# Transposed attention output, norm_ffn multiplied on the gathered rows with held weight loads, and x also given transposed

## The chip, the core and the metric

The kernel runs on one core of a Trainium2 chip. The metric is device time in microseconds (us) for one execution; the time before is the median of three runs. Five engines run side by side: PE (TensorE, matrix products and transposes), DVE (VectorE), ACT (ScalarE), POOL (GpSimd) and SP (SyncE, which here issues loads). Each engine runs its own instructions in order; they wait for one another and for DMA transfers by semaphores. PEld is the weight load of PE.

## The reference, cut to what is computed

One encoder block on 1024 tokens of width 1024:

```python
h = rms_norm(x, norm_mix)
z = h @ w_in                       # u | q | k | v, 512 columns each
A = multiscale_pool(u)             # 4 groups, windows 2/4/8/16
B = neighbourhood_attention(q, k, v)   # 8 heads of 64, a 16x64 grid of tokens
x = x + concat(A, B) @ w_out
h = rms_norm(x, norm_ffn)
aff = softmax(h @ w_router)        # 16 experts
gates, idx = top_k(aff.T, 128)     # each expert takes 128 tokens
ye = (silu(h[idx] @ w_gate) * (h[idx] @ w_up)) @ w_down
x = x + scatter_add(ye * gates)
x = x + sigmoid(rms_norm(x, norm_ple) @ w_ple_gate) * rms_norm(p @ w_ple_proj, norm_ple_post)
```

Everything is fp32.

## The kernel before, in words

A large product is made of three fast ones: both operands are split into a rounded part `hi` (ACT) and the rest `lo` (DVE, `split`, L83 to 88), and `mm3` (L90 to 97) issues hi·hi, lo·hi and hi·lo. So every weight and activation passes ACT and DVE once before PE can use it. PE's order is written out by hand: `run_block` issues the 8 groups of a product (k = 0 to 7), and ahead of group i the small pieces that a table gives for position i (8 stands behind the last group). PE therefore waits wherever a piece's input is late, and what stands behind the piece waits too. DVE, ACT and POOL are ordered by a scheduler. The stages:

1. **First projection** (u, L189 to 198). The tokens come in 8 groups u of 128 (16 grid rows by 8 columns). `load_x0` brings x by rows, `norm_x` takes the sum of squares, `turn_x` (L179) turns x by 8 PE transposes into PSUM and splits from there.
2. **Attention** in 32 blocks t = (pair of heads pr, group u). `pair_block` (L295) projects q, k and v of block t; beside it `side_at` (L407) puts `score` of block t-3 at position 0, its `turn_p` at 5 and 6 and its `blend` at 7 and 8, and `turn_qk` of block t-1 at 6. `score` (L334) multiplies q and k of two heads on the two row halves of the array (64 rows each); DVE adds the bias and finds the maximum, ACT takes exp and its sum. `turn_p` transposes the weights of a head (2 or 3 key groups of 128), and `blend` (L368) multiplies them by v: 128 tokens by 64 channels for each head, in plain fp32, then DVE takes the reciprocal of the sums and scales into `yas`, by tokens.
3. **Output projection and routing** for 8 row blocks (`out_block`). `prep` (L448) makes the transposed input `ct` of a block; the attention half is turned by 4 PE transposes per block into the PSUM buffer "t" and split. The last three attention blocks finish inside the first two output blocks. `route` computes the router's softmax; then `gained` (L531) multiplies the block's 1024 columns by norm_ffn on POOL and the row is stored in `hrow` with its affinities. Meanwhile DVE ranks the affinities (L580 to 631), and PE transposes `at` for it, in the same PSUM buffer "t".
4. **End of routing**: the last block's softmax and `gained`, the last ranking steps, the token lists, and the gather of expert 0's 128 rows (L928); beside it the units of `embed` (p @ w_ple_proj).
5. **Experts**: 16 of them, each 24 weight chunks of 1 MB (`load_chunk`), loaded by SP into raw slots of several pools (A 8, B 4, C 3, O, H), split by ACT and DVE into at most 4 `fhi`/`flo` pairs, used by 12 matmuls of 512 columns. Each expert's rows are gathered by POOL during the one before.
6. **Gate stage**, with norm_ple_post applied on DVE.

Of the kernel before, what the change touches and what calls it, by code (L numbers as in the profile page):

```python
# [41 lines left out]
NRC = 3  # L42
# [4 lines left out]
def block_kernel(ctx, tc, x, p, vecs, w_u_in, w_qkv, w_pool, bias_rows, w_out, w_router, w_gate, w_up,  # L47
# [118 lines left out]

    def load_x0(u):
        xts[u] = up.tile([P, D], F32, tag="x", name=f"x_{u}", bufs=3)
        for c in (slice(0, 512), slice(512, D)) if u == 0 else (slice(0, D),):
            SP.dma_start(xts[u][:, c], x_u[u][..., c])  # L170

    def norm_x(u):
        xt = xts[u]
        sq = up.tile([P, D], BF16, tag="sq", name=f"sq_{u}", bufs=1)
# [37 lines left out]
    load_x0(0)  # L212
# [17 lines left out]
    for u in range(NU):  # L230
        sides = {}
        if u + 1 < NU:
            sides[4] = [lambda u=u: turn_x(u + 1, 0)]
            sides[6] = [lambda u=u: turn_x(u + 1, 1)]
        if u:
            sides[3] = [lambda u=u: turn_u(u - 1)]
        if u + 1 < NU:
            sides.setdefault(6, []).append(lambda u=u: norm_x(u + 1))
        run_block(u_block(u), sides)
        if u + 3 < NU:  # L240
            load_x0(u + 3)
# [46 lines left out]
    vs, qs, qkns, sbs, PTs, pys, dens = {}, {}, {}, {}, {}, {}, {}  # L288
# [45 lines left out]
    def score(t):  # L334
# [72 lines left out]
    def side_at(t):  # L407
        sides = {}

        def at(i, f, *a):  # L410
            sides.setdefault(i, []).append(lambda: f(*a))
        if t == 0:
            at(4, turn_u, NU - 1)
        if t >= 3:
            at(0, score, t - 3)
            at(5, turn_p, t - 3, 0)
            at(6, turn_p, t - 3, 1)
            at(7, blend, t - 3, 0)
            at(8, blend, t - 3, 1)
        if 1 <= t <= NT:  # L420
            at(6, turn_qk, t - 1)
        return sides
# [25 lines left out]
    def prep(u):  # L448
# [67 lines left out]
    def softmax(u):  # L516
# [233 lines left out]
    for u in range(NU):  # L750
# [4 lines left out]
        if u == 0:  # L755
            at(0, score, NT - 3)
            at(2, turn_p, NT - 3, 0)
            at(2, turn_p, NT - 3, 1)
            at(3, turn_qk, NT - 1)
            at(4, blend, NT - 3, 0)  # L760
            at(4, blend, NT - 3, 1)
            at(4, score, NT - 2)
            at(6, turn_p, NT - 2, 0)
            at(6, turn_p, NT - 2, 1)
            at(6, score, NT - 1)
            at(7, blend, NT - 2, 0)
            at(7, blend, NT - 2, 1)
            at(8, turn_p, NT - 1, 0)
            at(8, turn_p, NT - 1, 1)
# [12 lines left out]
        if u == 1:  # L782
# [29 lines left out]
    fps = fps_st.enter_context(pool("fps", 2, space=PSUM))  # L812
    units = embed_units()
# [95 lines left out]
    def index(e):  # L909
# [15 lines left out]
        if e == 0:  # L925
# [3 lines left out]
                                      in_offset=bass.IndirectOffsetOnAxis(ap=ix[:, :1], axis=0))  # L929
        xes[e] = xe  # L930
# [98 lines left out]
    for e in range(E):  # L1029
# [16 lines left out]
        for kk in range(8):  # L1046
# [70 lines left out]
_INS = ['x', 'p', 'vecs', 'w_u_in', 'w_qkv', 'w_pool', 'bias_rows', 'w_out', 'w_router', 'w_gate', 'w_up',  # L1117
# [78 lines left out]
```

## Time and profile before

| what | us |
|---|---|
| median of 3 runs (lowest, highest) | 1672.84 (1672.43, 1674.53) |
| the profiled execution, its own time | 1677.14 |
| span of its trace | 1675.4 |
| PE, PEld busy | 1637.1, 1372.4 |
| DVE, ACT, POOL busy | 1347.9, 1152.5, 171.7 |
| mean granted clock of TensorE | 0.995 |

The profiled execution ran 1.74 us outside its span and 4.3 us over the median. Busy time of PE counts matmuls as the profile models them, which overlap; so the distance from one start to the next tells what an instruction costs in a run of them. The chain of waits that ended last lies on PE for 87% of the span.

### The profile page before, as it was taken

To read this page: it belongs to the slowest core of one execution; us is meant where nothing else is said; L and a number is where in the kernel's file an instruction comes from. 1 tells how busy PE (TensorE), PEld (TensorE's weight loads), DVE (VectorE), ACT (ScalarE), POOL (GpSimd) and SP (SyncE) were. 2 spreads that over 40 slices of the span, in tenths; PEclk is the share of its full clock that TensorE was granted. 3 is DMA by queue.
4 is the path that set the end of the run, shared out by engine and by line. 5 is a ranking of instruction groups with operands and counts; after the bars stand their busy time and mean duration, and the time that the engine had idled before them with its cause. 6 is when DMAs were issued, how large, how long until landed. Compare 5 with 4: busy or idle time off the path is not lost.

```text
span 1675.4 us, 22979 instructions
## 1 busy us (share of the span) xinstructions
PE 1637.1 (98%) x8181; PEld 1372.4 (82%) x8181; DVE 1347.9 (80%) x1870; ACT 1152.5 (69%) x1472; POOL 171.7 (10%) x215
## 2 busy tenths in 40 slices
PE   8999999998899999999999999999999999999998
PEld 6889998787778888888888888888888888888787
DVE  4474555448879999999999999999999999999932
ACT  6254555432388888888888888888888888888631
POOL 1111112243220000000000000000000000000200
PEclk9999999999999999999999999999999999999999
DMA  6301201263689999999999999999999999999121
GB/s 182 121 20 41 67 26 51 59 220 102 205 315 397 379 368 407 372 390 387 369 402 376 372 404 369 398 380 366 409 368 395 384 367 405 375 382 394 51 100 59
DMA packets 129266, 470.54 MB, mean 281 GB/s; under 512 B 9600, under 2 KB 14720, under 8 KB 129152
## 3 DMA queue, kind: packets, MB, share of 16 engines
q1 hardware_dynamic: 123120, 446.85, 70.8%
q0 software_dynamic: 6032, 22.23, 5.1%
q8 instruction: 64, 1.05, 0.3%
q14 instruction: 50, 0.41, 0.1%
HBM read 448.00 MB, written 21.04 MB: 280 GB/s over the span
## 4 chain that ended last, share of the span: by engine, by line
PE 87%; DVE 7%; POOL 1%; ACT 1%; issue 1%; DMA 1%; SPq 0%; DVEq 0%; ACTq 0%; POOLq 0%
PE pu L93 8%; PE pu L95 8%; PE pu L97 8%; PE pg L93 7%; PE pg L95 7%; PE pg L97 7%; PE pd L95 7%; PE pd L93 7%; PE pd L97 7%; PE proj L93 2%; DVE both L580 2%; PE proj L97 2%; PE proj L95 2%; PE py L374 2%; PE tr_h L937 2%; PE pq L95 2%
## 5 line engine op out<-in xcount | busy, mean ns | idle before, releaser
L86 DVE TENSOR_TENSOR flo<-fraw,fhi 128x1024 fp32r<-128x1024 f32 x766 | 913.6, 1221 | 70.2 <-ACT fhi L85 33.5
L85 ACT ACTIVATE fhi<-fraw 128x1024 fp32r<-128x1024 f32 x766 | 807.1, 1060 | 191.5 <-PE pd L95 71.7
L93 PE MATMUL pd<-fhi,hidT 128*128 128x512 f32 x508 | 160.9, 398 | 0.0
L93 PE MATMUL pg<-fhi,xeT 128*128 128x512 f32 x512 | 159.2, 392 | 0.8 <-ACT xeT L85 0.8
L93 PE MATMUL pu<-fhi,xeT 128*128 128x512 f32 x512 | 159.2, 392 | 0.0
L95 PE MATMUL pu<-fhi,xeT 128*128 128x512 f32 x512 | 158.0, 390 | 0.0
L95 PE MATMUL pg<-fhi,xeT 128*128 128x512 f32 x512 | 157.8, 389 | 0.0
L97 PE MATMUL pg<-flo,xeT 128*128 128x512 f32 x512 | 157.8, 389 | 0.0
L97 PE MATMUL pu<-flo,xeT 128*128 128x512 f32 x512 | 157.6, 389 | 0.0
L95 PE MATMUL pd<-fhi,hidT 128*128 128x512 f32 x508 | 157.1, 391 | 0.0
L97 PE MATMUL pd<-flo,hidT 128*128 128x512 f32 x508 | 156.8, 390 | 0.0
L97 PEld LDWEIGHTS pu<-flo,xeT 128*128 128x128 f32 x512 | 96.1, 188 | 20.4
L95 PEld LDWEIGHTS pg<-fhi,xeT 128*128 128x128 f32 x512 | 96.0, 188 | 20.4 <-DVE xeT L86 0.4
L95 PEld LDWEIGHTS pu<-fhi,xeT 128*128 128x128 f32 x512 | 96.1, 188 | 20.3
L97 PEld LDWEIGHTS pg<-flo,xeT 128*128 128x128 f32 x512 | 96.1, 188 | 20.1
L97 PEld LDWEIGHTS pd<-flo,hidT 128*128 128x128 f32 x508 | 95.3, 188 | 20.6
L95 PEld LDWEIGHTS pd<-fhi,hidT 128*128 128x128 f32 x508 | 95.3, 188 | 20.5
L93 PEld LDWEIGHTS pg<-fhi,xeT 128*128 128x128 f32 x512 | 94.8, 188 | 19.8 <-ACT xeT L85 1.1
L93 PEld LDWEIGHTS pu<-fhi,xeT 128*128 128x128 f32 x512 | 94.9, 188 | 18.8
L93 PEld LDWEIGHTS pd<-fhi,hidT 128*128 128x128 f32 x508 | 92.0, 188 | 16.4
L1022 POOL DMA_INDIRECT acc_rows<-ye,ix x16 | 26.6, 1660 | 764.3 <-ACT ye L1009 699.2
L93 PE MATMUL proj<-wph,xT 128*128 128x384 f32 x256 | 100.3, 392 | 0.0
(235 smaller groups left out, 2365.9 us busy)
## 6 DMA issues: line engine op xcount, KB each, us to landing
fraw<-in_w_gate_dram SPq DMA_DIRECT2D x128, 1024.0 KB, 7.3
fraw<-in_w_down_dram SPq DMA_DIRECT2D x128, 1024.0 KB, 9.3
fraw<-in_w_up_dram SPq DMA_DIRECT2D x127, 1024.0 KB, 7.7
x<-in_x_dram SPq DMA_DIRECT2D x15, 512.0 KB, 5.1
wp_raw<-in_w_qkv_dram SPq DMA_DIRECT2D x16, 384.0 KB, 4.0
h_rows<-x POOLq DMA_DIRECT2D x8, 520.5 KB, 3.8
wo_raw<-in_w_out_dram SPq DMA_DIRECT2D x8, 512.0 KB, 3.3
acc_rows<-x SPq DMA_DIRECT2D x8, 512.0 KB, 4.2
```

Of the source, the lines that this page charges most:

```text
L85: ACT.activation(hi, src, AF.Copy)
L86: return DVE.tensor_tensor(lo, src, hi.bitcast(F32), op=ALU.subtract)
L93: PE.matmul(outs[j], xh, wh[j], start=start, stop=False)
L95: PE.matmul(outs[j], xl, wh[j], start=False, stop=False)
L97: PE.matmul(outs[j], xh, wl[j], start=False, stop=stop)
L374: PE.matmul(pys[t][:, h], PTs[t, h][:, j * P:(j + 1) * P], vs[NU * pr + u0 + j][:, h * HD:(h + 1) * HD], start=(j == 0), stop=(j == u1 - u ...
L580: DVE.tensor_tensor(b[:, :, j], a[:, :, 0], a[:, :, 1], op=(ALU.max, ALU.min)[j])
L937: PE.transpose(pt[:, j, :], src[:, k * P:(k + 1) * P], ident)
L1022: return POOL.indirect_dma_start(out=acc, out_offset=bass.IndirectOffsetOnAxis(ap=idxs[e][:, :1], axis=0), in_=ye, in_offset=None, compute ...
```

## The change

- The host gives x a second time, transposed (`xt`). Each u loads both forms; `turn_x` splits straight from the loaded tile with no transposes. x itself serves the sum of squares alone, squared in place. The x buffers go from 3 to 2, the x loads of group u+2 follow block u.
- `blend` swaps its operands: v is the weight (128 rows, 64 columns), the transposed attention weights are the moving side (128 columns), and the two heads alternate on the two column halves of the array. Its output is already transposed, so `prep` splits it from SBUF. The division by the sums moves ahead of `turn_p`: per head a reciprocal and a `tensor_scalar` over the 128x384 weights on DVE; `ya` becomes a copy. Each piece gets one more block: `blend` of t-5 and `score` of t-3 at 1, `turn_p` of t-4 at 5 and 6, `turn_qk` at 7.
- `gained` is gone. The gathered rows are multiplied by norm_ffn in two halves of 512 columns, on DVE for expert 0 and on POOL for the 15 others. norm_ffn and norm_ple_post get buffers of their own; pool C has 2 slots.
- Weight loads: 4 A chunks are loaded in output block 2 (3 before) and then CCHH (CCCHH). None is issued between these and the token list of expert 0 (4 were, two of them behind `counted`); 4 follow it, and 4 further ones and norm_ple_post wait for a small transfer that reads the gathered rows of expert 0.
- A tile `bank_order` holds the order of the PSUM banks.

```diff
+    def load_xT(u):
+        raw_xT[u] = up.tile([P, KD, P], F32, tag="xr", name=f"xr_{u}")
+        n = 2 if u == 0 else 1
+        for h in range(n):
+            ks = slice(h * KD // n, (h + 1) * KD // n)
+            SP.dma_start(raw_xT[u][:, ks], xt[u][:, ks])
...
-        ACT.activation(sq, xt, AF.Square, accum_out=ssq)
+        ACT.activation(xts[u], xts[u], AF.Square, accum_out=ssq)
...
-        pt = ps.tile([P, 4, P], F32, tag="pt", name=f"xt_ps_{u}_{h}")
-        for k in range(4):
-            PE.transpose(pt[:, k, :], xts[u][:, (4 * h + k) * P:(4 * h + k + 1) * P], ident)
-        split(xT[u][:, 0, 4 * h:4 * h + 4], xT[u][:, 1, 4 * h:4 * h + 4], pt)
+        ks = slice(4 * h, 4 * h + 4)
+        split(xT[u][:, 0, ks], xT[u][:, 1, ks], raw_xT[u][:, ks])
...
             ACT.activation(sb[:, :n], sb[:, :n], AF.Exp, bias=nmx, scale=-1.0, accum_out=dens[t][:, h:h + 1])
+            rd = tiny.tile([P, 1], F32, tag="rd", name=f"rd_{pr}_{u}_{h}")
+            DVE.reciprocal(rd, dens[t][:, h:h + 1])
+            DVE.tensor_scalar(sb[:, :n], sb[:, :n], rd, None, op0=ALU.mult)
...
         for j in range(u1 - u0):
-            PE.matmul(pys[t][:, h], PTs[t, h][:, j * P:(j + 1) * P],
-                      vs[NU * pr + u0 + j][:, h * HD:(h + 1) * HD], start=(j == 0), stop=(j == u1 - u0 - 1))
-        if h == 1:
-            rd = tiny.tile([P, 2], F32, tag="rd", name=f"rd_{pr}_{u}")
-            DVE.reciprocal(rd, dens[t])
-            DVE.tensor_tensor(yas[u // 4][:, u % 4, pr * P:(pr + 1) * P].rearrange("p (a b) -> p a b", b=HD), pys[t],
-                              rd[:, :, None].to_broadcast([P, 2, HD]), op=ALU.mult)
+            for h in range(2):
+                hs = slice(h * HD, (h + 1) * HD)
+                PE.matmul(py[hs], vs[NU * pr + u0 + j][:, hs], PTs[t, h][:, j * P:(j + 1) * P],
+                          start=(j == 0), stop=(j == u1 - u0 - 1))
+        DVE.tensor_copy(yas[u // 4][:, u % 4, pr * P:(pr + 1) * P], py)
...
-            at(0, score, t - 3)
-            at(5, turn_p, t - 3, 0)
...
+                at(1, blend, t - 5)
+            at(1, score, t - 3)
...
-        pt = ps.tile([P, 4, P], F32, tag="t", name=f"yat_{u}", bufs=1)
-        for k in range(4):
-            PE.transpose(pt[:, k, :], yas[u // 4][:, u % 4, k * P:(k + 1) * P], ident)
-        split(ct[:, 0, 4:8], ct[:, 1, 4:8], pt)
+        split(ct[:, 0, 4:8], ct[:, 1, 4:8], yas[u // 4][:, u % 4].rearrange("p (k q) -> p k q", q=P))
...
-        gained(u)
         POOL.tensor_copy(x1s[u][:, D:D + E], affq[:, u, 0:E])
...
-    for which in "CCCHH":
+    gfb, gp = (fw.tile([P, D], F32, name=n) for n in ("gfb", "gp"))
+    bc_rows(gfb, norm_ffn[0], D)
+    for which in "CCHH":
         load_chunk(which)
-    ring += ["A"] * 5
...
-    with tc.issue_after(counted.ins):
-        feed()
-        feed()
...
+        for h in range(2):
+            hs = slice(h * 512, (h + 1) * 512)
+            (POOL if e else DVE).tensor_tensor(xe[:, hs], xe[:, hs], gfb[:, hs], op=ALU.mult)
...
+    mark = SP.dma_start(nc.dram_tensor("mark", (1, 16), F32, kind="Internal").ap(), xes[0][0:1, D:D + 16])
+    with tc.issue_after(mark.ins):
+        for _ in range(4):
+            load_chunk("A")
+        bc_rows(gp, norm_ple_post[0], D)
...
     with tc.issue_after(made.ins):
-        feed()
-        feed()
+        for _ in range(4):
+            feed()
```

The order of PE at the seam of two attention blocks, before (`py` is the blend, `s` the score, `proj` the projection; the names' last numbers are buffers):

```order
L374 MATMUL py_6_1383<-v_5_1043,PT_6_0_1361 128x64 [waits Activation_49]
L374 MATMUL py_6_1383<-v_6_1128,PT_6_0_1361 128x64
L374 MATMUL py_6_1383<-v_7_1213,PT_6_0_1361 128x64
L93 MATMUL proj_1_1322<-wph_3_1232,xT_208 128x384
L95 MATMUL proj_1_1322<-wph_3_1232,xT_208 128x384
L97 MATMUL proj_1_1322<-wpl_3_1233,xT_208 128x384
L374 MATMUL py_6_1383<-v_5_1043,PT_6_1_1370 128x64 [waits DVE_49]
L374 MATMUL py_6_1383<-v_6_1128,PT_6_1_1370 128x64
L374 MATMUL py_6_1383<-v_7_1213,PT_6_1_1370 128x64
L345 MATMUL s_7_0_1408<-kT,q_7_1291 128x256
```

and the same place in the changed kernel:

```order
L95 MATMUL proj_1_2711<-wph_0_2158,xT_199 128x384
L97 MATMUL proj_1_2711<-wpl_0_2159,xT_199 128x384
L384 MATMUL py_4_2715<-PT_4_0_2676,v_3_2255 64x128 [waits DVE_49,Activation_49]
L384 MATMUL py_4_2715<-PT_4_1_2685,v_3_2255 64x128 [waits DVE_49]
L384 MATMUL py_4_2715<-PT_4_0_2676,v_4_2341 64x128
L384 MATMUL py_4_2715<-PT_4_1_2685,v_4_2341 64x128
L384 MATMUL py_4_2715<-PT_4_0_2676,v_5_2427 64x128
L384 MATMUL py_4_2715<-PT_4_1_2685,v_5_2427 64x128
L351 MATMUL s_6_0_2724<-kT,q_6_2588 128x384 [waits Activation_49]
```

The two heads' products stood apart, each of them two key groups or three in a row with a group of `proj` between; now they alternate, three key groups by two heads, straight ahead of the score.

The order of PE where the output projection begins, before (`yat` is the transposed attention output, `po` the output projection):

```order
L374 MATMUL py_4_3299<-v_3_2966,PT_4_1_3286 128x64 [waits DVE_49]
L374 MATMUL py_4_3299<-v_4_3057,PT_4_1_3286 128x64
L374 MATMUL py_4_3299<-v_5_3139,PT_4_1_3286 128x64
L461 MATMUL yat_3351<-ident,ya_88 128x128 [waits DVE_49]
L461 MATMUL yat_3351<-ident,ya_88 128x128 x3
L345 MATMUL s_5_0_3361<-kT,q_5_3209 128x384 [waits Activation_49]
L345 MATMUL s_5_1_3362<-kT,q_5_3209 128x384
L345 MATMUL s_5_0_3361<-kT,q_5_3209 128x384
L345 MATMUL s_5_1_3362<-kT,q_5_3209 128x384
L345 MATMUL s_5_0_3361<-kT,q_5_3209 128x384
L345 MATMUL s_5_1_3362<-kT,q_5_3209 128x384
L93 MATMUL po_0_3358<-woh_2808,ct_3346 128x512 [waits Activation_49]
```

and in the changed kernel:

```order
L93 MATMUL proj_7_3252<-wph_3_2616,xT_515 128x384
L95 MATMUL proj_7_3252<-wph_3_2616,xT_515 128x384
L97 MATMUL proj_7_3252<-wpl_3_2617,xT_515 128x384
L93 MATMUL po_0_3369<-woh_2800,ct_3362 128x512 [waits PE_49,Activation_49]
L93 MATMUL po_1_3370<-woh_2800,ct_3362 128x512 [waits DVE_49,PE_49]
L95 MATMUL po_0_3369<-woh_2800,ct_3362 128x512 [waits Pool_49]
```

Blend, transposes and score that stood between the last `proj` and the first `po` are gone from there; both `po` buffers have the PSUM tag of `proj`.

The order of POOL at the gathers of experts 1 and 2, before:

```order
L928 DMA xe_5122<-h_rows,ix_5120 128x1041 [waits DVE_49]
L1022 DMA acc_rows<-ye_5550,ix_4883 1024x1024 [waits Activation_49]
L928 DMA xe_5724<-h_rows,ix_5722 128x1041 [waits DMASW0_49,DVE_49]
L1022 DMA acc_rows<-ye_6152,ix_5120 1024x1024 [waits DMASW3_49,Activation_49]
L928 DMA xe_6326<-h_rows,ix_6324 128x1041 [waits DMASW2_49,DVE_49]
```

and in the changed kernel:

```order
L923 DMA xe_5134<-h_rows,ix_5132 128x1041 [waits DVE_49]
L927 TENSOR_TENSOR xe_5134<-xe_5134,gfb 128x512 [waits DMAHW7_49,DMASW2_49]
L927 TENSOR_TENSOR xe_5134<-xe_5134,gfb 128x512
L1025 DMA acc_rows<-ye_5564,ix_4873 1024x1024 [waits DMAHW3_49,DMAHW5_49,DMAHW2_49,Activation_49]
L923 DMA xe_5738<-h_rows,ix_5736 128x1041 [waits DMAHW2_49,DMASW0_49,DVE_49]
L927 TENSOR_TENSOR xe_5738<-xe_5738,gfb 128x512 [waits DMASW4_49]
L927 TENSOR_TENSOR xe_5738<-xe_5738,gfb 128x512
```

Behind each gather stand two multiplications that wait for it to land, and the scatter of the expert before stands behind them.

## Rows read from the trace of the kernel before

**Rows 1.** Windows by stage: length, busy time of each engine (x instructions), PEclk, DMA share, GB/s

```profile
8.90:69.00 60.10, 56.24 (x277) 45.19 (x278) 24.89 (x46) 29.62 (x52) 5.96 (x16) 0.97 0.48 129
69.00:307.60 238.60, 228.99 (x1503) 211.50 (x1502) 137.12 (x377) 121.27 (x313) 42.67 (x62) 0.99 0.15 49
307.60:442.40 134.80, 124.22 (x661) 102.43 (x660) 90.64 (x357) 40.22 (x98) 43.66 (x54) 0.97 0.48 138
442.40:475.10 32.70, 29.97 (x154) 23.64 (x154) 23.34 (x98) 22.83 (x37) 13.21 (x24) 0.95 0.78 273
475.10:1572.00 1096.90, 1096.89 (x5120) 906.90 (x5120) 1025.27 (x931) 904.59 (x918) 52.03 (x32) 1.00 0.99 377
```

**Rows 2.** Waits of PE: line, awaited: us in total, times, longest us

```profile
PE pt L360 <- ACT sb L352: 7.2, 7, 2.0
PE at L589 <- DVE ct L86: 5.7, 3, 2.4
PE qkt L320 <- DVE qkn L312: 2.7, 2, 1.4
...
PE xt_ps L184 <- DMA x<-in_x_dram: 1.6, 1, 1.6
...
PE po L93 <- DVE qkn L312: 1.4, 1, 1.4
```

**Rows 3.** Groups by line, 8.9 to 69 us

```profile
L184 PE MATMUL xt_ps<-ident,x 128*128 128x128 f32 x56 | 8.4, 273 | 1.6 <-DMA x<-in_x_dram 1.6
```

**Rows 4.** Timeline of PE, 37.5 to 40.5 us: start, length, instruction

```profile
38.58 0.40 PE L97 MATMUL pu<-wul,xT 128*128 128x512 f32 x1
38.81 0.60 PE L184 MATMUL xt_ps<-ident,x 128*128 128x128 f32 x4
...
39.49 0.39 PE L95 MATMUL pu<-wuh,xT 128*128 128x512 f32 x1
```

**Rows 5.** Timeline of PE, 288.3 to 292.3 us

```profile
288.44 0.49 PE L360 MATMUL pt<-ident,sb 128*128 128x128 f32 x3
288.77 0.38 PE L320 MATMUL qkt<-ident,qkn 128*128 128x128 f32 x2
...
289.52 0.78 PE L374 MATMUL py<-v,PT 128*128 128x64 f32 x6
290.10 0.42 PE L93 MATMUL proj<-wph,xT 128*128 128x384 f32 x1
...
290.71 0.78 PE L374 MATMUL py<-v,PT 128*128 128x64 f32 x6
291.42 0.79 PE L345 MATMUL s<-kT,q 64*128 64x384 f32 x6
292.14 0.44 PE L93 MATMUL proj<-wph,xT 128*128 128x384 f32 x1
```

**Rows 6.** Timeline of PE, 266.5 to 268.2 us

```profile
266.62 0.62 PE L345 MATMUL s<-kT,q 64*128 64x256 f32 x6
267.17 0.44 PE L93 MATMUL proj<-wph,xT 128*128 128x384 f32 x1
```

**Rows 7.** Groups by line and shape, 69 to 307 us

```profile
L374 PEld LDWEIGHTS py<-v,PT 128*128 128x128 f32 x314 | 43.1, 192 | 0.6 <-ACT PT L363 0.3
...
L365 DVE COPY PT<-pt 128x384 f32<-128x384 f32 x22 | 12.2, 556 | 17.2 <-PE pt L360 17.2
...
L378 DVE RECIPROCAL rd<-den 128x2 f32<-128x2 f32 x29 | 4.8, 164 | 18.2 <-ACT sb L352 18.2
```

**Rows 8.** Line 533, `gained`: duration ns min/median/max, first and last start

```profile
L533 POOL TENSOR_TENSOR x<-x,gfb x8: 2378/2392/2435, 337.9 to 449.6; 128x1024 f32<-128x1024 f32 x8
```

**Rows 9.** Timeline of DVE, 382.2 to 387.5 us

```profile
382.69 2.09 DVE L526 TENSOR_SCALAR both<-ex,sm 128x16 f32<-128x16 f32 x1
```

**Rows 10.** Timeline of DVE, 449.1 to 453 us

```profile
449.19 0.22 DVE L526 TENSOR_SCALAR both<-ex,sm 128x16 f32<-128x16 f32 x1
```

**Rows 11.** The page's groups: busy, mean ns, idle time before

```profile
L86 DVE TENSOR_TENSOR flo<-fraw,fhi 128x1024 fp32r<-128x1024 f32 x766 | 913.6, 1221 | 70.2 <-ACT fhi L85 33.5
```

More of the change, by code (lines that the diff above doesn't have):

```diff
@@ L41, with block_kernel @@
 NRB = 4
-NRC = 3
+NRC = 2
 NH = 4
 @with_exitstack
-def block_kernel(ctx, tc, x, p, vecs, w_u_in, w_qkv, w_pool, bias_rows, w_out, w_router, w_gate, w_up,
+def block_kernel(ctx, tc, x, xt, p, vecs, w_u_in, w_qkv, w_pool, bias_rows, w_out, w_router, w_gate, w_up,
                  w_down, w_ple_gate, w_ple_proj, norm_ffn, norm_ple_post, edge, consts, out):
@@ L165, in load_u_w @@
         uwt.append((hi, lo))
+    raw_xT = {}
+    def load_xT(u):
[4 more added lines that the diff above has]
+            SP.dma_start(raw_xT[u][:, ks], xt[u][:, ks])
     def load_x0(u):
-        xts[u] = up.tile([P, D], F32, tag="x", name=f"x_{u}", bufs=3)
-        for c in (slice(0, 512), slice(512, D)) if u == 0 else (slice(0, D),):
-            SP.dma_start(xts[u][:, c], x_u[u][..., c])
+        xts[u] = up.tile([P, D], F32, tag="x", name=f"x_{u}")
+        SP.dma_start(xts[u], x_u[u])
     def norm_x(u):
-        xt = xts[u]
-        sq = up.tile([P, D], BF16, tag="sq", name=f"sq_{u}", bufs=1)
         ssq = tiny.tile([P, 1], F32, tag="ssq", name=f"ssq_{u}")
-        ACT.activation(sq, xt, AF.Square, accum_out=ssq)
+        ACT.activation(xts[u], xts[u], AF.Square, accum_out=ssq)
         rstd_of(ssq, D, 1, f"rstd_{u}", rx[:, u:u + 1])
@@ L211, in block_kernel @@
         POOL.memset(Us[i][:, :, S + PAD:], 0.0)
-    load_x0(0)
+    load_xT(0)
     SP.dma_start(vec, vecs)
@@ L222, in block_kernel @@
         load_u_w(kk)
-    load_x0(1)
+    load_x0(0)
     norm_x(0)
     first.close()
-    load_x0(2)
+    load_xT(1)
+    load_x0(1)
     cst = up.tile([P, 4 * P], F32, name="cst", bufs=1)
@@ L239, in block_kernel @@
         run_block(u_block(u), sides)
-        if u + 3 < NU:
-            load_x0(u + 3)
+        if u + 2 < NU:
+            load_xT(u + 2)
+            load_x0(u + 2)
         if u == 3:
@@ L286, in pool_mix @@
         ACT.activation(Ug, pp, AF.Copy, scale=pscale[:, g:g + 1])
-    vs, qs, qkns, sbs, PTs, pys, dens = {}, {}, {}, {}, {}, {}, {}
+    vs, qs, qkns, sbs, PTs, dens = {}, {}, {}, {}, {}, {}
     bias_t = {}
@@ L366, in turn_p, with blend @@
         PTs[t, h] = PT
-    def blend(t, h):
+    def blend(t):
         pr, u = divmod(t, NU)
         u0, u1, n = span(u)
-        if h == 0:
-            pys[t] = ps.tile([P, 2, HD], F32, tag="py", name=f"py_{pr}_{u}", bufs=1)
+        py = ps.tile([P, P], F32, tag="py", name=f"py_{pr}_{u}", bufs=1)
         for j in range(u1 - u0):
-            PE.matmul(pys[t][:, h], PTs[t, h][:, j * P:(j + 1) * P],
-                      vs[NU * pr + u0 + j][:, h * HD:(h + 1) * HD], start=(j == 0), stop=(j == u1 - u0 - 1))
-        if h == 1:
-            rd = tiny.tile([P, 2], F32, tag="rd", name=f"rd_{pr}_{u}")
-            DVE.reciprocal(rd, dens[t])
-            DVE.tensor_tensor(yas[u // 4][:, u % 4, pr * P:(pr + 1) * P].rearrange("p (a b) -> p a b", b=HD), pys[t],
-                              rd[:, :, None].to_broadcast([P, 2, HD]), op=ALU.mult)
+            for h in range(2):
[3 more added lines that the diff above has]
+        DVE.tensor_copy(yas[u // 4][:, u % 4, pr * P:(pr + 1) * P], py)
     wo = []
@@ L414, in side_at @@
         if t >= 3:
-            at(0, score, t - 3)
-            at(5, turn_p, t - 3, 0)
[L417 to L421, printed above, removed]
+            if t >= 5:
+                at(1, blend, t - 5)
+            at(1, score, t - 3)
+        if t >= 4:
+            at(5, turn_p, t - 4, 0)
+            at(6, turn_p, t - 4, 1)
+        if t >= 1:
+            at(7, turn_qk, t - 1)
         return sides
@@ L526, in softmax @@
         DVE.tensor_scalar(affq[:, u, 0:E], ex, sm, None, op0=ALU.mult)
-        gained(u)
         POOL.tensor_copy(x1s[u][:, D:D + E], affq[:, u, 0:E])
         POOL.dma_start(hrow_u[u], x1s[u][:, :ROW])
-    def gained(u):
-        rows = x1s[u][:, :D]
-        POOL.tensor_tensor(rows, rows, gfb[0], op=ALU.mult)
     def route(u):
@@ L755, in block_kernel @@
         if u == 0:
[L756 to L761, printed above, removed]
-            at(4, score, NT - 2)
[L763 to L769, printed above, removed]
+            at(1, blend, NT - 5)
+            at(1, score, NT - 3)
+            at(2, turn_qk, NT - 1)
+            at(2, turn_p, NT - 4, 0)
+            at(3, turn_p, NT - 4, 1)
+            at(4, blend, NT - 4)
+            at(4, score, NT - 2)
+            at(5, turn_p, NT - 3, 0)
+            at(5, turn_p, NT - 3, 1)
+            at(7, blend, NT - 3)
+            at(7, score, NT - 1)
+            at(8, turn_p, NT - 2, 0)
+            at(8, turn_p, NT - 2, 1)
         elif u < NU - 1:
@@ L775, in block_kernel @@
         if u == 1:
-            at(1, blend, NT - 1, 0)
-            at(1, blend, NT - 1, 1)
+            at(0, blend, NT - 2)
+            at(1, turn_p, NT - 1, 0)
+            at(1, turn_p, NT - 1, 1)
+            at(3, blend, NT - 1)
         if u + 1 < NU:
@@ L787, in swap @@
                 load_side()
-            at(2, swap)
+            at(3, swap)
         if u == 2:
@@ L791, in block_kernel @@
             at(4, split_side, "pj")
-            at(6, lambda: [load_chunk("A") for _ in range(NRA - 5)])
+            at(6, lambda: [load_chunk("A") for _ in range(NRA - 4)])
         if 3 <= u < NU - 1:
@@ L812, in block_kernel @@
     fps = fps_st.enter_context(pool("fps", 2, space=PSUM))
+    fps.tile([P, 2, 512], F32, tag="pg", name="bank_order", bufs=1)
     units = embed_units()
@@ L1055, in block_kernel @@
                 ahead[0] = (NH + 2, NH + 4, 0)[kk - 3]
-            if e == E - 1 and kk == 1:
-                gp = slot_tile(ring.pop(0), "g_post")[:, 0]
-                bc_rows(gp, norm_ple_post[0], D)
     warm2 = tiny.tile([P, 1], F32, tag="warm2", name="warm2")
@@ L1114, in block_kernel @@
     order.close()
[L1117 removed]
+_INS = ['x', 'xt', 'p', 'vecs', 'w_u_in', 'w_qkv', 'w_pool', 'bias_rows', 'w_out', 'w_router', 'w_gate', 'w_up',
         'w_down', 'w_ple_gate', 'w_ple_proj', 'norm_ffn', 'norm_ple_post', 'edge', 'consts']
@@ L1179 @@
     inputs['p'] = inputs['p'][0, 0].T
+    inputs['xt'] = inputs['x'][0].reshape(GR, NU, UC, KD, P).transpose(1, 4, 3, 0, 2).reshape(NU, P, KD, P)
     inputs['edge'] = _edge()
```

3 lines of the change are left out of this document (removed).

## The prediction

> **What bounds the kernel now.** I read the windows by stage first [rows 1]. Compare the length of a stage with the time for which PE was busy: the experts take 1096.9 us and PE has not 0.1 us free in them, so nothing but fewer or faster matmuls shortens that stage. Ahead of it PE is idle for 3.9, 9.6, 10.6 and 2.7 us in the four stages, 26.8 us in all, and its granted clock is below 1.00: 0.97, 0.99, 0.97 and 0.95. One less the clock, times the length, is the time lost to half speed, the lower of the levels 1.2 and 2.4 GHz: 1.8, 2.4, 4.0 and 1.6 us. So there are two things to win: PE's own instructions, and up to some 36 us of idle time and low clock. The waits of PE [rows 2] name the idle time: `pt`, the transposes of the attention weights, waits 7.2 us for exp, `at`, the ranking's transposes, 5.7 us for the DVE half of a split. Then I priced single instructions by the distance from one start to the next in the timeline [rows 4 to 6].
>
> **Part 1, x also transposed.** Removed from the stream of PE: 56 transposes [rows 3], 14 groups of 4. Such a group and the one matmul behind it take 39.49 - 38.81 = 0.68 us, and the matmul takes 0.23 of that (38.81 - 38.58) [rows 4]; so 0.45 for a group and 6.3 us for 14. The 1.6 us for which they waited for x of group 1 [rows 2] go, but xT of group 1 now stands behind x of group 0 on SP, one 512 KB transfer later than x did; I put the two at nothing. ACT no longer waits for PSUM here, which should give back about half of the other 2.3 us of idle time. Cover: the x bytes double, by 4 MB; the stage moved 129 GB/s at a DMA share of 0.48 over 60.1 us [rows 1], which is 7.8 MB, so the share rises to about 0.73. If SP is held by the two buffers, that cover is gone. I take -7.5 us, ends -10 and -4.
>
> **Part 2, the blend.** Before: six records of `py` for a head (three fp32 products, two records each), 290.10 - 289.52 = 0.58 us for the first head and 291.42 - 290.71 = 0.71 for the second, ahead of the score: 1.29 a block [rows 5]. Now there are still 12 records, each with 128 moving columns instead of 64. Three transposes of 128 fp32 columns take 288.77 - 288.44 = 0.33, so 0.11 for one [rows 5]. Whether two column halves run together no row shows. The nearest is the score, on two row halves: six matmuls take 0.72 us at 384 columns [rows 5] and 0.55 at 256 [rows 6]. The difference of 0.17 is three times 128 columns at 0.23 for 512, not six times; so the halves run in pairs, and 0.55 - 3 x 0.115 = 0.2 is what going into that tiling and out of it costs, 0.1 a change. By this row the new blend, whose order pairs the last record of one product with the first of the next, takes 7 x 0.11 + 0.1 (one change more than before) = 0.87: 0.42 less. At the edges, with two key groups, 0.86 falls to 5 x 0.11 + 0.1 = 0.65. 24 blocks and 8 edges: -10.1 - 1.7 = **-11.8 us**. If the halves run one after the other, 12 x 0.11 + 0.1 = 1.42, and 0.98 at the edges: +4.1. I take -11.8, as the rows of the score are nearest, and keep +4.1 for the range.
>
> **Part 3, one more block of slack in attention.** `turn_p` no longer stands in the block of its own score, so most of the 7.2 us of `pt` goes (I take 6), and of the 2.7 of `qkt`, now a group later, 1 us; of the clock lost after such stops 1.5 of 2.4. Added is DVE work for each block: two reciprocals at 0.16 instead of one, and two multiplications of 128x384. No row has one of these; 0.22 for 128x16 [rows 10] and 0.56 for a copy of 128x384 out of PSUM [rows 7] bound it, and I take 0.45: about 1.0 us a block, 32 us in all, on a DVE busy for 137 of 238.6 us [rows 1]. It fits, but DVE waits in order for exp ahead of them, and what stands behind (the `lo` of keys and queries) is late next: +2 us of new waits. Sum -6.5, ends -11 and +1.
>
> **Part 4, output projection and routing.** Removed: eight groups of four transposes of `yat`, 8 x 0.45 = -3.6. Removed too: `gained`, 2.39 us on POOL, eight times [rows 8]. Its price is on DVE: a `tensor_scalar` of 128x16 issued while it runs took 2.09 us [rows 9] and 0.22 otherwise [rows 10], so POOL holds DVE up for its length, some 8 x 1.9 = 15 us of a DVE busy for 90.6 of 134.8 us. With it, and with the buffer "t" no longer shared, the waits of `at` lose their cause: I take -4.5 of 5.7, and -2.5 of the 4.0 us of low clock. Added: the second `po` waited 1.4 us for the buffer of the last `proj` [rows 2] with a score (0.72) and four transposes (0.45) in between; these are gone, so +1.2. The blend of block 30 now stands right behind its own weights' transposes, up to +0.8. Sum **-8.6**, ends -13 and -4.
>
> **Part 5, gather and weight loads.** The last `gained` lies on the way to the token lists, and the two chunks behind `counted` are off DVE there; against that, expert 0's rows are multiplied on DVE ahead of their transposes, one pass of 1024 columns, about the 1.22 of a `flo` [rows 11]. PE is idle for only 2.7 us of this stage, as `embed` fills it. I take -2, ends -4 and +1.5.
>
> **Part 6, experts.** Per expert POOL multiplies 1024 columns, 2.39 us as `gained` did [rows 8], and holds DVE up meanwhile. DVE is busy for 1025.3 of 1096.9 us [rows 1], so idle for 4.5 us per expert; 2.4 of these go. Its `flo` waits for `fhi` and so for PE's buffers [rows 11], which says that it runs ahead of PE. I take 0, and the bounds are in the rivals. One raw slot fewer costs nothing: loads wait for slots that `flo` frees, and 13 are left.
>
> **Sum.** -7.5 - 11.8 - 6.5 - 8.6 - 2 = -36.4 us, on the profiled execution's 1677.1: 1640.7. That one ran 4.3 us over the median, so the median should be 1672.8 - 36.4 = **1636.4 us**.
>
> **Rivals.**
> - *Column halves take turns* (0.18): the score speaks against it, but it uses row halves. +15.9: 1652.
> - *Weight loads in the open* (0.05), the slower side: if each of the 12 records of a blend had to wait for its own load, at half of the 0.192 us of a `py` load [rows 7], a blend would take 12 x 0.21 + 0.1 = 2.6, +1.3 a block, about +40 over 32 blocks, in place of -11.8: 1688. It decides from 0.07 us of open load per record. Against it: `py` records with such loads start 0.58 / 6 = 0.097 apart [rows 5], so their loads of 0.192 overlap other work already. The Trainium skill says (TensorE: Matmul & The Clock Gate, Part 3: Packing small matmuls, The mechanism) that a weight load overlaps running matmuls only where the row group differs. By that rule this rival would win, since all these products use all 128 rows, and the time would be its 1688; the `py` rows before the change, 0.097 against 0.192, disagree with the rule.
> - *POOL starves PE in the experts* (0.14): each multiplication stops `flo` for 2.4 us. A stop of 1 us that reaches PE 15 times gives +15: 1651. Were each one 3.6 us (two halves of 1.2 and a `flo` behind them), +54 would make 1690, slower than before from 2.7 us each; I give that end 0.03 of the 0.14. For it: DVE is busy for 93% there. Against it: its waits for `fhi`.
> - *DVE holds attention back* (0.09): the multiplications put exp, reciprocal and product in line, and `pt` waits as before. Part 3 gives +3 instead of -6.5: 1646.
>
> **How the numbers follow.** My forecast has 0.54. Its own ends reach from about 1622 to 1648; with the halves in turn, and POOL's 1 us, the time lies near 1652, and a part of both near 1660. The range 1621 to 1660 leaves out the slow ends and some mixtures. A measurement of this kernel tells 0.2%, 3.3 us, from no change. Faster by more: 0.87, all cases but the slow ends and heavy mixtures; within: 0.05; slower: 0.08, the two ends above.
>
> **What would show it.** The steps are right if the first `proj` starts about 7 us earlier; if `py` and `s` together take about 1.6 us in a block where before 1.29 + 0.72 = 2.0 stood; if `pt` and `at` lose their waits and a `both` of DVE is no longer 2 us long between 337 and 450; and if the experts still take 1096.9 us with no idle PE. I am wrong if twelve `py` records need over 1.3 us, if a wait of `pg`, `pu` or `pd` for `flo` shows up behind each multiplication of `xe`, or if x comes too late for two or more groups.

## The result, and the profile after

The change makes the kernel faster: median 1645.49 us (1639.46 to 1648.15, 4 runs) against 1673.37 (4 runs), a ratio of 0.9829 with a 95% interval of 0.9805 to 0.9853. That is 27.9 us, inside the range, and 8.5 us less than the 36.4 that were forecast. The profiled execution after took 1648.15 us, span 1646.4, granted clock 0.993. Of the four executions the fastest has a granted clock of 0.997, the others 0.992 or 0.993.

The windows of the changed kernel by stage, with the columns of [rows 1]; the cuts are the first `pu`, `proj`, `po`, `pg` and `pq`:

```profile
7.90:68.40 60.50, 52.67 (x220) 41.42 (x221) 24.50 (x46) 30.02 (x52) 5.93 (x16) 0.97 0.74 194
68.40:287.70 219.30, 215.25 (x1476) 187.91 (x1474) 156.24 (x464) 115.29 (x315) 43.16 (x62) 0.99 0.17 54
287.70:444.20 156.50, 149.21 (x809) 121.57 (x809) 106.03 (x464) 62.08 (x132) 40.47 (x70) 0.98 0.53 164
444.20:1545.50 1101.30, 1100.98 (x5129) 910.01 (x5129) 1045.00 (x933) 905.51 (x920) 117.46 (x62) 1.00 0.99 377
```

The same five starts of both kernels, from their timelines of PE, show where the time went:

| from the first ... to the first ... | before, us | after, us | difference | forecast (parts) |
|---|---|---|---|---|
| `pu` to `proj` (first projection) | 60.07 | 60.55 | +0.5 | -7.5 (1) |
| `proj` to `po` (attention) | 240.16 | 219.27 | -20.9 | -18.3 (2, 3) |
| `po` to `pg` (output projection, routing) | 165.99 | 156.56 | -9.4 | -10.6 (4, 5) |
| `pg` to `pq` (experts) | 1099.26 | 1101.23 | +2.0 | 0 (6) |

The first `pu` starts 1.0 us earlier, and the stretch behind the experts differs by 0.1. The second and third rows need a correction, as work changed sides. Ahead of the first `po` stood the blends of 29 blocks before (320 of the 352 `py` records) and of 27 now (296), the scores of 30 and 29, and the weights' transposes of 29 and 28. At 0.89, 0.72 and 0.66 us a block some 3.2 us of attention have moved into the third row. The second row also lost the first `yat` (0.5 us) and gained a wait of the first `po` for `ct` (1.4), which both belong to part 4. Put right by this estimate, attention gave 18.6 us and the rest up to `pg` 11.7.

The first line of the windows tells of something wrong: PE works for 52.67 us there, 3.6 less than before, and yet the stage is no shorter. The waits of PE in the changed kernel name what took its place [rows 2 before]:

```profile
PE ut L207 <- ACT us L201: 6.7, 5, 2.3
...
PE po L93 <- DVE qkn L318: 2.0, 1, 2.0
PE pg L93 <- ACT xeT L85: 1.8, 1, 1.8
...
PE s L351 <- DVE kT L333: 1.5, 1, 1.5
...
PE po L93 <- ACT ct L464: 1.4, 1, 1.4
PE py L384 <- DVE PT L374: 1.2, 2, 1.0
```

`pt` and `at` are gone from the list, as forecast. At its head now stands `ut`, which waited 1.3 us before: the transposes of the finished u, which wait for `us`, ACT's copy out of PSUM that scales by the row sums of x. ACT's timeline in the changed kernel shows what `us` waits for:

```profile
40.87 1.15 ACT L85 ACTIVATE xT<-xr 128x512 fp32r<-128x512 f32 x2 [1.23 <-DMA xr<-in_xt_dram]
41.93 0.67 ACT L201 ACTIVATE us<-pu,rx 128x512 f32<-128x512 f32 x1
43.10 1.06 ACT L182 ACTIVATE x<-x 128x1024 f32<-128x1024 f32 x1 [0.51 <-DMA x<-in_x_dram]
...
46.40 1.16 ACT L85 ACTIVATE xT<-xr 128x512 fp32r<-128x512 f32 x2 [1.13 <-DMA xr<-in_xt_dram]
48.85 1.06 ACT L182 ACTIVATE x<-x 128x1024 f32<-128x1024 f32 x1 [1.30 <-DMA x<-in_x_dram]
...
50.41 0.67 ACT L201 ACTIVATE us<-pu,rx 128x512 f32<-128x512 f32 x1
```

The `us` at 50.41 is that of group 4 (they count from 0 to 7). Ahead of it in ACT's queue stand the Squares of groups 6 and 7 (43.10, 48.85) and the split of xT of group 7 (46.40), each idle until its own transfer landed. The share of DMA over the stage is 0.74, beside 0.73 forecast, but from 20 to 40 us it is 1.02. So two readings stood against each other: the transfers are too slow (A), or they run ahead of PE, and ACT's order hands their wait on to PE (C).

### The profile page after: what moved, and what is told of

It is laid out like the page before. It is cut to its first block, busy times and chain, and to the rows that moved or that the text cites. A ratio compares the mean times of both kernels' runs of the same rounds, so it can differ in the third digit from the quotient of the medians.

```text
span 1646.4 us, 22882 instructions
## 1 busy us (share of the span) xinstructions
PE 1616.0 (98%) x8085; PEld 1341.2 (81%) x8085; DVE 1377.4 (84%) x1968; ACT 1146.6 (70%) x1472; POOL 218.8 (13%) x237
## 4 chain that ended last, share of the span: by engine, by line
PE 92%; DVE 3%; DMA 2%; POOL 1%; ACT 1%; issue 1%; SPq 0%; DVEq 0%; ACTq 0%; POOLq 0%
PE pu L93 7%; PE pu L95 7%; PE pu L97 7%; PE pg L93 7%; PE pg L97 7%; PE pg L95 7%; PE pd L95 7%; PE pd L93 7%; PE pd L97 7%; PE proj L93 3%; DMA x<-in_x_dram 2%; PE proj L97 2%; PE proj L95 2%; PE po L93 2%; PE tr_h L935 2%; PE po L95 2%
## 5 line engine op out<-in xcount | busy, mean ns | idle before, releaser
L86 DVE TENSOR_TENSOR flo<-fraw,fhi 128x1024 fp32r<-128x1024 f32 x766 | 932.2, 1255 | 54.1 <-ACT fhi L85 28.4
L97 PEld LDWEIGHTS pg<-flo,xeT 128*128 128x128 f32 x512 | 96.7, 189 | 20.3
L97 PEld LDWEIGHTS pu<-flo,xeT 128*128 128x128 f32 x512 | 96.1, 188 | 20.3
L95 PEld LDWEIGHTS pu<-fhi,xeT 128*128 128x128 f32 x512 | 96.1, 188 | 20.3
```

Source lines behind the costliest of these rows:

```text
L86: return DVE.tensor_tensor(lo, src, hi.bitcast(F32), op=ALU.subtract)
L95: PE.matmul(outs[j], xl, wh[j], start=False, stop=False)
L97: PE.matmul(outs[j], xh, wl[j], start=False, stop=stop)
```

## The experiments

All are edits of the changed kernel, and differences are told against its 1645.5 us. The ratios in brackets are to the kernel of before as it ran beside each of them (1674.0 to 1674.4 us).

**x turned by PE again.** Line for line the first projection of before (its loads, its Square and its three x buffers are not printed here):

```diff
-        split(xT[u][:, 0, ks], xT[u][:, 1, ks], raw_xT[u][:, ks])
+        for k in range(4):
+            PE.transpose(pt[:, k, :], xts[u][:, (4 * h + k) * P:(4 * h + k + 1) * P], ident)
+        split(xT[u][:, 0, 4 * h:4 * h + 4], xT[u][:, 1, 4 * h:4 * h + 4], pt)
```

> The changed kernel with its first projection undone: x by rows alone, turned by PE as before. In the changed kernel the first `proj` starts at 68.41 us against 68.96 before, so part 1 gave almost nothing. Theory A (the doubled x bytes take back what the 14 groups of transposes gave, as `ut` waits 6.7 us for the row sums): first `proj` at 68 to 70 us, the total within 3 us of the changed kernel, 1642 to 1649 us. Theory B (part 1 as predicted, and some other delay sits in the stage of both kernels' common code): without xt the stage grows by 5 us or more, total 1650 to 1654 us.

Measured: 1647.2 us (ratio 0.9846, 0.983 to 0.9861), first `proj` at 67.66. The two intervals overlap: as put in the changed kernel, xt is worth nothing that shows. Theory B of this run falls. Theory A has the total; its start of 68 to 70 us is missed by 0.3, and its reason, the bytes, falls with the runs below.

**`ut` later.**

```diff
-        if u:
-            sides[3] = [lambda u=u: turn_u(u - 1)]
+        if u >= 2:
+            sides[7] = [lambda u=u: turn_u(u - 2)]
+        if u == NU - 1:
+            sides[8] = [lambda u=u: turn_u(u - 1)]
```

> The changed kernel with the transposes `ut` of group u moved from position 3 of block u+1 to position 7 of block u+2 (PE's order alone). Theory A (only the row sums are late: x by rows lands behind xT, and PE stops at `ut` in order): the waits of `ut` go from 6.7 us to under 1.5, the first `proj` starts at 60 to 62 us, the total falls by 5 to 8 us against the changed kernel. Theory B (the transfers as a whole are late, xT too): the waits move to `pu` for xT, the first `proj` stays above 66 us, the total within 2 us of the changed kernel.

Measured: 1639.1 us (0.98, 0.9784 to 0.9816), first `proj` at 61.91. The waits of `ut` are gone; 3.4 us of waits of `pu` for `us` (the PSUM buffer) have come. xT itself is early enough. Theory A.

**The weights' loads behind x.**

```diff
-        if 2 <= u < 6:
-            load_pair_w(0, u - 2)
+        if u == 5:
+            for kk in range(4):
+                load_pair_w(0, kk)
```

> The changed kernel with the four loads of the first pair's qkv weights moved behind the last x load (1.5 MB out of the stretch of 25 to 42 us). Theory A (bandwidth: the DMA engines are busy at a share of 1.0 from 10 to 52 us, so every byte taken away there brings x earlier): x lands about 5 us earlier at the end of the stage, the waits of `ut` fall from 6.7 to 2 to 4 us, total 2 to 5 us lower than the changed kernel. Theory B (the two x buffers and the round of Square, release and next load are the limit, not bytes): waits of `ut` 5 us or more, total within 2 us.

Measured: 1643.2 us (0.9814, 0.98 to 0.9827), first `proj` at 68.39, waits of `ut` 5.6 us, one of them 3.8. Taking 1.5 MB away from the stretch left the stage as long as it was. Theory A falls: the bytes were not the limit. Of theory B the waits came, and the total misses it by 0.3 us. Neither names ACT's order.

**ACT in the order of the program text.** The scheduler had put ACT up to two groups further ahead than the text; here it is held to the text, in which `us` of group u follows the Square of group u+1:

```diff
+    acts = ExitStack()
+    acts.enter_context(tc.manual_schedule(engines={mybir.EngineType.Activation}))
     for u in range(NU):
...
+    acts.close()
     xst.close()
```

> The changed kernel with ACT held to the order of the program text in the loop of the first projection: the copy `us` of group u stands behind the split and the Square of group u+1 only, in place of those of group u+2. Theory C (the transfers run ahead of PE; PE waits because `us` stands in ACT's queue behind two further groups, each waiting for its x to land): the waits of `ut` fall from 6.7 us to under 1, the first `proj` starts at 59 to 62 us, the total 6 to 9 us under the changed kernel, although x and xT are loaded at the same rate. Theory A (row sums late by bytes alone): waits of `ut` 4 us or more, total within 2 us.

Measured: 1638.5 us (0.9787, 0.9773 to 0.98), first `proj` at 59.83, one wait of `ut` of 0.29 left. ACT's timeline of this run shows the new order:

```profile
26.16 1.15 ACT L85 ACTIVATE xT<-xr 128x512 fp32r<-128x512 f32 x2 [0.48 <-DMA xr<-in_xt_dram]
27.78 1.06 ACT L182 ACTIVATE x<-x 128x1024 f32<-128x1024 f32 x1 [0.46 <-DMA x<-in_x_dram]
28.74 0.18 ACT L182 ACTIVATION_READ_ACCUMULATOR x<-x 128x1 f32 x1
30.51 0.69 ACT L201 ACTIVATE us<-pu,rx 128x512 f32<-128x512 f32 x1 [1.58 <-PE pu L97]
```

Now `us` is idle until PE, not until DMA. The share of DMA from 20 to 40 us is still 0.98 there: the same transfers, and no wait.

**The control: turned by PE, and ACT in that order.** The two edits above together.

> The changed kernel with x by rows alone and turned by PE, and with ACT in the order of the program text in the first projection: the control for the run with ACT in order. Theory A (the transposes cost what was read, 14 groups by 0.45 us and their waits, and xt gives it back once ACT's order lets it): first `proj` at 66 to 68 us, 6 to 8 us behind that run's 59.83, total 1644 to 1647 us. Theory B (ACT's order is the whole gain, with or without xt): first `proj` at 60 to 63 us, total within 2 us of 1638.5.

Measured: 1645.0 us (0.9825, 0.981 to 0.984), first `proj` at 67.83. So ACT's order alone gives nothing that shows. With ACT in order, xt gives 6.4 us of the stretch from `pu` to `proj` (58.80 here, 52.44 there) and 6.4 of the total; the other 1.6 of the 8.0 us between the two starts lie ahead of the first `pu` (9.03 and 7.39). Theory A holds: 14 groups of transposes at 0.45 us were read as 6.3.

**The heads' products in turn.**

```diff
-        for j in range(u1 - u0):
-            for h in range(2):
+        for h in range(2):
+            for j in range(u1 - u0):
```

> The changed kernel with the blend's products in another order: the two or three of one head, then those of the other, in place of alternating heads. Theory A (the column halves run in pairs because neighbours in the order use different halves): the 12 `py` records that take 0.80 us (246.99 to 247.79) take 1.3 to 1.4, 24 blocks by 0.55 and 8 by 0.35 make 14 to 16 us more than the changed kernel, about 1660 us. Theory B (the records are cheaper for another reason, such as half as wide weight loads): the same 0.8 us and the same total within 3 us.

Measured: 1648.5 us (0.9848, 0.9833 to 0.9863). PE's timeline of the changed kernel, then of this run:

```profile
246.72 0.34 PE L97 MATMUL proj<-wpl,xT 128*128 128x384 f32 x1
246.99 0.88 PE L384 MATMUL py<-PT,v 128*64 128x128 f32 x12
247.79 0.62 PE L351 MATMUL s<-kT,q 64*128 64x256 f32 x6
```

```profile
247.23 0.34 PE L97 MATMUL proj<-wpl,xT 128*128 128x384 f32 x1
247.50 1.14 PE L384 MATMUL py<-PT,v 128*64 128x128 f32 x12
248.57 0.62 PE L351 MATMUL s<-kT,q 64*128 64x256 f32 x6
```

Twelve records take 0.80 us alternating and 1.07 in turn, so the alternating order is worth a quarter; but 12 in turn were expected at 1.3 to 1.4. With two key groups both orders take 0.59, which neither theory says. 24 blocks by 0.27 make 6.5 us, of which 3 to 4 show in the stretch from `proj` to `po` (222.4 against 218.1 to 219.3 in runs that leave the blend alone). Half of theory A. Whether the two halves run at the same time, or the order only spares a wait between two products that add into the same place, no run tells apart.

**The old lag.** Score, `turn_p` and blend of t-3 in one block again, with the multiplication kept on the way. The pieces inside the first output blocks go back with them (not printed here):

```diff
-            if t >= 5:
-                at(1, blend, t - 5)
-            at(1, score, t - 3)
-        if t >= 4:
-            at(5, turn_p, t - 4, 0)
-            at(6, turn_p, t - 4, 1)
+            at(0, score, t - 3)
+            at(5, turn_p, t - 3, 0)
+            at(6, turn_p, t - 3, 1)
+            at(8, blend, t - 3)
...
```

> The changed kernel with the attention pieces at their old places (score of t-3 at 0, its `turn_p` at 5 and 6, its blend at 8, `turn_qk` at 6), all else kept, so reciprocal and multiplication stand in the same block between exp and `turn_p`. Theory A (the block of slack is what takes the waits of `pt` away): waits of `pt` come back with 10 us or more, the stretch from the first `proj` to the first `po` grows from 219.3 to 228 to 240 us, total 8 to 20 us over the changed kernel. Theory B (the gain there is the blend's): waits of `pt` under 5 us, total within 4 us.

Measured: 1665.8 us (0.9948, 0.9933 to 0.9964). The stretch from `proj` to `po` takes 245.7 us, 26.5 more; the one from `po` to `pg` takes 151.9, 4.7 less, as fewer pieces are left for it. So 21.8 us in both, and 20.3 in the total. PE's waits in this run:

```profile
PE pt L369 <- DVE rd L360: 18.5, 17, 2.7
...
PE pt L369 <- DVE sb L361: 3.8, 5, 2.1
```

Theory A, by a little more than its upper ends. Without the extra block, moving the division ahead of the transposes would have cost more than the blend gives.

**`gained` back on the row blocks**, with the weight loads of before:

```diff
+        gained(u)
+    def gained(u):
+        rows = x1s[u][:, :D]
+        POOL.tensor_tensor(rows, rows, gfb[0], op=ALU.mult)
...
-            (POOL if e else DVE).tensor_tensor(xe[:, hs], xe[:, hs], gfb[:, hs], op=ALU.mult)
```

> The changed kernel with `gained` back on the 8 row blocks and the weight loads as before the change (pool C with 3 slots, norm_ffn and norm_ple_post in slots of the ring), parts 1 to 3 and the split without transposes kept. Theory A (POOL's `gained` holds DVE up, and that reaches PE): eight DVE instructions of 2 us or more come back, waits of `at` of 2 to 5 us, the stretch from the first `po` to the first `pg` grows from 156.6 to 161 to 165 us, the experts' stretch shrinks from 1101.2 to 1099; total 3 to 7 us over the changed kernel. Theory B (the waits of `at` came from the buffer shared with `yat` alone): no wait of `at`, the total at or under the changed kernel, by up to 2 us.

Measured: 1652.6 us (0.9871, 0.9856 to 0.9886); from `po` to `pg` 165.2 us, from `pg` to `pq` 1098.6. The ranking's `both` on DVE, all 214 of them, duration min/median/max in ns: first the changed kernel, then this run.

```profile
L579 DVE TENSOR_TENSOR both<-both x214: 171/206/347, 366.2 to 428.2; 32x64 f32<-32x64 f32 x77, 64x32 f32<-64x32 f32 x30
```

```profile
L584 DVE TENSOR_TENSOR both<-both x214: 171/206/2428, 368.4 to 438.1; 32x64 f32<-32x64 f32 x77, 64x32 f32<-64x32 f32 x30
```

The longest falls from 2428 to 347 ns where POOL has no `gained`. With it PE waits 3.9 us at `at`, for `both`, although the buffer is not shared here, so theory B falls. Theory A has the waits and the experts; stretch and total lie 0.2 and 0.1 us over its upper ends.

**The gathered rows multiplied on DVE for all experts.**

```diff
-            (POOL if e else DVE).tensor_tensor(xe[:, hs], xe[:, hs], gfb[:, hs], op=ALU.mult)
+            DVE.tensor_tensor(xe[:, hs], xe[:, hs], gfb[:, hs], op=ALU.mult)
```

> The changed kernel with the gathered rows multiplied on DVE for all experts. In the changed kernel POOL's two multiplications of an expert take 3.5 to 11.4 us from start to end, and the mean `flo` of DVE 1255 ns in place of 1221. Theory A (none of this reaches PE; the 2.0 us by which the experts' stretch is longer come from a low clock at its start): `flo` mean back to 1220 to 1230 ns, the stretch from the first `pg` to the first `pq` within 1 us of 1101.2, total within 2 us. Theory B (POOL's hold of DVE costs PE some 0.13 us an expert): that stretch 1099 to 1099.5, total 2 us lower.

Measured: 1772.2 us (1.0584, 1.0568 to 1.06). Both theories missed it: the price is not the multiplication but the wait ahead of it. DVE's timeline of this run:

```profile
543.65 0.15 DVE L912 TENSOR_REDUCE ix<-pi 128x1 int32<-128x2 f32 x1
551.62 1.29 DVE L927 TENSOR_TENSOR xe<-xe,gfb 128x512 f32<-128x512 f32 x2 [7.82 <-DMA xe<-h_rows,ix]
552.83 2.35 DVE L86 TENSOR_TENSOR flo<-fraw,fhi 128x1024 fp32r<-128x1024 f32 x2
```

The multiplication stands right behind the list of rows that starts the gather, and DVE idles 7.8 us until the rows land; the `flo` behind it come late, and PE's waits in this run have

```profile
PE pg L97 <- DVE flo L86: 94.3, 15, 7.6
```

and a granted clock of 0.964 over the run. On POOL the same wait holds up nothing that PE waits for. What it does there, in the changed kernel:

```profile
L927 POOL TENSOR_TENSOR xe<-xe,gfb x30: 1293/2275/9199, 480.6 to 1437.5; 128x512 f32<-128x512 f32 x30
```

**Chunk loads issued earlier**: the four held ones when the counts are known.

```diff
+    with tc.issue_after(counted.ins):
+        for _ in range(4):
+            load_chunk("A")
...
     with tc.issue_after(mark.ins):
-        for _ in range(4):
-            load_chunk("A")
```

> The changed kernel with its four held chunk loads issued when the counts are known, some 10 us ahead of the gather of expert 0, in place of after it has landed. Theory A (the hold is worth little: the gather before the change landed 5.3 us after its issue with loads running, now 5.0): the gather lands 5 to 6 us after its issue, the first `pg` at most 1 us later, total within 2 us of the changed kernel. Theory B (free DMA engines are what the gather needs): it lands 7 us or more after its issue, total 2 us or more over the changed kernel.

Measured: 1643.4 us (0.9821, 0.9801 to 0.9842). The rows landed 5.3 us after the gather's issue (433.82 to 439.12), 5.0 in the changed kernel, and `po` to `pg` takes 156.3 us. The hold is worth nothing that shows.

**A version that beats both.** ACT in order, and at the start of the output projection blend and score ahead of the first `po`:

```diff
-            at(1, blend, NT - 5)
-            at(1, score, NT - 3)
+            at(0, blend, NT - 5)
+            at(0, score, NT - 3)
...
-            at(0, blend, NT - 2)
+            at(1, blend, NT - 2)
             at(1, turn_p, NT - 1, 0)
```

> The changed kernel with ACT in order, and at the start of the output projection blend and score ahead of the first `po` (position 0 in place of 1), and blend of block 30 one group later. Theory A (the first two `po` wait 1.4 and 2.0 us, and `py` 1.6 us, because nothing of their length stands between): these waits fall by 2 to 4 us in sum, with some low clock behind them; the stretch from the first `po` to the first `pg` shrinks from 155.5 to 151 to 154 us, total 2 to 4 us under 1638.5. Theory B (the score moved ahead waits for its keys instead): a wait of `s` of 1 to 2 us appears, total within 1.5 us.

Measured: 1633.2 us (1631.2 to 1634.6, 5 runs; 0.9754, 0.974 to 0.9767), 40 us below the kernel before and 5 below ACT in order alone. The stretch from `po` to `pg` is 152.9 us (155.5 there), while that from `proj` to `po` stays at 218.2 although blend and score now lie in it. So 2.6 us are explained; the profiled executions differ by 0.9, as the first `proj` came 1.7 us later in this one, and the rest of the 5 us is not accounted for. The wait of `po` for `ct` is gone, that for `qkn` is still 1.9. No wait of `s` has come beside the 1.5 that all these runs have.

## Why the prediction was right, and where it was off

**Part 1 is the step that failed in size.** The forecast said that "ACT no longer waits for PSUM here, which should give back about half of the other 2.3 us", and named SP's buffers as what could take the cover away. The transposes cost what [rows 4] said, 6.4 us by the control. With ACT in the text's order the stage from `pu` to `proj` takes 59.83 - 7.39 = 52.4 us, 7.6 less than before, beside -7.5 forecast; as the change stood, it took 0.5 more than before. What was missed is that a load for every group turned ACT into a queue of DMA waits, and that the scheduler had put `us` behind those of up to two further groups. By the prediction's own sign, x too late for two or more groups, this part was wrong: `ut` waited five times. The forecast argued from the order of SP and PE in this stage, and the answer stood in that of ACT. The rise of the share to 0.74 was right and told nothing, as an average over a stage that is full from 10 to 40 us (1.05 and 1.02) and nearly idle from 52 to 60 (0.04).

**Part 2.** Forecast 0.87 us a block, an extra change of tiling included. Measured 0.80 for the records, and 0.27 from the last `proj` to the first record, where two records of `proj` lie 0.18 apart: 0.89 in all. At two key groups 0.59 + 0.09 = 0.68 against 0.65. The price of one record was read too high (0.11 from the transposes; in turn they take 1.07 / 12 = 0.089), and the gain of alternating halves too high; that the two errors cancel is luck. So alternating does help, as the score's rows suggested, only less. The rival of weight loads in the open is out: records start 0.067 us apart with loads of 0.137 (median), all of them over the same 128 rows. The rule of the Trainium skill that the rival was weighed by (TensorE: Matmul & The Clock Gate, Part 3: Packing small matmuls, The mechanism) does not hold for this blend.

**Part 3.** Parts 2 and 3 together gave about 18.6 us where 18.3 were forecast. The waits of `pt` fell from 7.2 to 0, more than the 6 taken, and DVE rose by 156.2 - 137.1 = 19 us in a stretch 19 us shorter. The multiplication takes 419 ns at 128x384, between the two bounds and near the 0.45 taken. New waits in the stretch are `s` 1.5 us and 0.2 of `py`, within the 2 allowed; 1.6 more of `py` fall behind the first `po`. The granted clock reads 0.99 before and after, so the 1.5 us taken for it do not show. The rival of DVE holding attention back did not come, but the old lag shows that it would have: 22 us of waits.

**Parts 4 and 5.** Forecast -10.6, measured -9.4, or about -11.7 with the moved work put back. That POOL's `gained` held DVE is shown (2428 ns against 347), and that this reached PE (3.9 us at `at`). The run that puts it back takes 8.7 us more (165.2 against 156.6) for `gained` and the weight loads of before together; how they share the rest was not tried, beyond the hold of four loads, which has no part in it. The second `po` was forecast to wait 2.6 us and waited 2.0; the wait of the first for `ct`, 1.4 us, was not in the sum.

**Part 6.** PE never waits for `flo`, so the slower rival is out, though the first three pairs on POOL took 11.4, 3.5 and 5.7 us from start to end: DVE's mean `flo` rose from 1221 to 1255 ns, its busy time by about 20 us, and it is still idle for 56 of 1101.3 us. The +2.0 us lie at the start, in the granted clock. In the first 10 us behind the first `pg` it is 0.70 in the changed kernel, 0.83 or 0.84 in six edits whose stretch takes 1099.9 to 1100.1, and 1.00 before (1099.3) and in the four that take 1098.6 to 1098.7, three of which leave this part as it is (the run with all rows on DVE is left aside). The wait of the first `pg` does not decide it: the old lag waits as long and keeps the full clock. The changed kernel, then the old lag, where pairs of `pg` start 0.85 and 0.47 apart:

```profile
444.24 1.22 PE L93 MATMUL pg<-fhi,xeT 128*128 128x512 f32 x2 [1.79 <-ACT xeT L85]
...
446.12 1.05 PE L97 MATMUL pg<-flo,xeT 128*128 128x512 f32 x2
446.97 1.05 PE L93 MATMUL pg<-fhi,xeT 128*128 128x512 f32 x2
```

```profile
465.42 0.73 PE L93 MATMUL pg<-fhi,xeT 128*128 128x512 f32 x2 [1.80 <-ACT xeT L85]
...
466.71 0.63 PE L97 MATMUL pg<-flo,xeT 128*128 128x512 f32 x2
467.18 0.62 PE L93 MATMUL pg<-fhi,xeT 128*128 128x512 f32 x2
```

At full clock the stretch is no longer than before, so the 0 of the forecast holds. What lowers the clock there stays open.

**The sum**, by the spans of the profiled executions, which fell by 29.0 where 36.4 were forecast: part 1 is 8.0 short, attention gave about 0.3 more, the stage behind it 1.1 more, the experts 2.0 less, and the first `pu` came 1.0 earlier. So the missing 7.4 us are about the size of part 1; the rest cancels.

## What to carry to other kernels

When a load is added, read the queue of the engine that consumes it, not only the one that issues it: ACT passed its waits for transfers on to everything behind them, and the scheduler's order had put there what PE needed next. A product that must wait for a gather belongs on an engine with nothing urgent behind it: here that mattered far more than what the product costs. An extra step on a chain wants its own block of lag: here the multiplication hardly showed with one, and the kernel took 20 us more without.

## What was not expected of the hardware

- Products on the two column halves of the array, 128 fp32 columns each, take 0.80 us for 12 records alternating and 1.07 in turn, but 0.59 for 8 in either order. Why the order makes no difference to eight stays open.
- POOL's multiplication of 128x512 beside a stream of `flo` takes 1.3 to 9.2 us (median 2.3), while `gained`, twice as wide, took 2.4 [rows 8] and stopped DVE. In the experts it is POOL that is stretched, and each `flo` lasts 1255 ns on average. What decides who waits was not tried.
- x by rows and by columns, with some weights between, came in at 254 to 258 GB/s at a share of 0.98 to 1.02 (20 to 40 us, ACT in order and the changed kernel), the experts' chunks at 377 GB/s at 0.99. A share near one is not one rate.
